# 512-wide products for the high weights of the MLPs, in a trunk of four layers

## The chip, the cores and the metric

The kernel runs on one core of a Trainium2 chip. The metric is the time of one execution on the device in microseconds (us); the profile is one such execution, taken by the hardware profiler. Its engines are TensorE (PE: matmuls into PSUM; PEld are its weight loads), VectorE (DVE), ScalarE (ACT), GpSimd (POOL) and the DMA queues, most of which SyncE (SP) issues.

## The reference

A decoder trunk of four layers over 256 tokens of 1024 features, all in fp32. Every layer is a mixer (S5, FoX attention, GLA, S5 again), an MLP and a gate ("PLE"), each on a normed copy of the residual stream `h`:

```python
def sqrelu_mlp(xn, w1, w2):
    return jnp.square(jax.nn.relu(xn @ w1)) @ w2          # w1: 1024 x 4096, w2: 4096 x 1024

for i in range(DEPTH):
    mixer, j = i % N_MIXERS, i // N_MIXERS
    xn = rmsnorm(h, norm_mix[i])
    y = ...                                               # s5, fox or gla
    h = h + y.astype(h.dtype)
    h = h + sqrelu_mlp(rmsnorm(h, norm_mlp[i]), mlp_w1[i], mlp_w2[i])
    gate = jax.nn.sigmoid(rmsnorm(h, norm_ple[i]) @ ple_gate[i])
    h = h + (p[i] @ ple_proj[i]) * gate
return rmsnorm(h, final_norm)
```

## The kernel before

`h` is kept transposed: features on the 128 partitions, the 256 tokens along the free axis, in four tiles `HH[n]` of 128 x 2 x 256. An fp32 product is made of three products of a narrower type: each operand is split into a high and a low part, and high x high, high x low and low x high are added up in PSUM. `col` issues these three, each 128 features by 256 tokens. `ktiles` holds an input in this form, high part `x[:, 0]` beside low part `x[:, 1]`, 256 tokens each.

Weights arrive as units of 256 x 512: `unit` fetches one (`raw`, on SP's queue), ScalarE casts its high part (`whi`), VectorE subtracts to get the low part (`wlo`). There are 3 buffers for `raw`, and 4 each for `whi` and `wlo`. A unit holds two blocks of 128 input features (`UK`) by four blocks `n` of 128 output features.

An MLP works through 8 blocks `c` of 512 of the 4096 inner features. For each, `dense` multiplies the input by a block of the first weight (four units) into two banks of PSUM with the tag `wk`, `relu2` makes the squared ReLU and splits it into high and low parts, and `second(c - 1)` multiplies the block before it by the second weight (two column halves `cb`, two units each) into four banks `y` (the tag `po` and three of `acc`), which stay open for the whole MLP. At the end `add` multiplies them by the norm's scale `r2` and adds them to `h`. PSUM has eight banks: three `acc`, three `wk`, one `po`, one `mk`. The norm's scale is applied behind the products, so its statistics run beside them: `rstd_rows` takes the mean of squares by a matmul with `mean`, `inverse_root` the root (on GpSimd's power, or a reciprocal on VectorE), `rstd` builds a diagonal tile `diag` on VectorE and spreads it over the partitions by a matmul with `ones`. `further` lets one step of the preparation of the last S5 layer run between blocks of an MLP (`s5_ahead`, in layers 0 to 2).

The gate `ple` calls `dense` with two banks of `acc` for its first column half and two of `wk` for its second, with `rstd_rows` and `rstd` called behind its second and third unit.

In the GLA mixer, `att` is a masked score tile of two chunks of 64 tokens; it is cleared on GpSimd, then the masked part of a PSUM bank is copied in by VectorE, and TensorE multiplies it with `v`. `oss` is GLA's own norm, whose power runs on GpSimd.

A scheduler sets the order on every engine from a simulated timeline, under the rule that a buffer of a pool (`BUFS` gives their numbers) is reused in turn. An engine works through its order strictly in sequence.

Of the kernel before, what the change touches and what calls it, by code (L numbers as in the profile page):

```python
# [18 lines left out]
EPS = 1e-6  # L19
UK = 2  # L20

BUFS = {"raw": 3, "wh": 4, "wl": 4, "x4": 4, "m4": 5, "win": 1, "c4": 6, "qo": 3, "tm": 3, "s2": 10, "a2": 4, "wt": 3, "g2": 3, "s1": 2,
        "acc": 3, "wk": 3, "po": 1, "mk": 1}


# [29 lines left out]
class Trunk:  # L55
# [60 lines left out]
            nc.gpsimd.affine_select(v, v, [[0, 4], [1, 64]], ALU.is_ge, 0, base=0, channel_multiplier=-1)  # L116


    def t1(self, name, shape=(128, T), dt=F32, tag="s1"):
        return self.sc.tile(list(shape), dt, name=name, tag=tag, bufs=BUFS[tag])  # L120

    def t2(self, name, shape=(128, 512), dt=F32, tag="s2"):
        return self.sc.tile(list(shape), dt, name=name, tag=tag, bufs=BUFS[tag])

# [50 lines left out]
    def dense(self, x, w, evac, cbs=(0, 1), scale=None, mid=None, tags=("acc", "acc")):  # L175


        nk = 2 * len(x)
        i = 0
        for cb in cbs:  # L180
            ps = [self.psum((128, 2, T), tags[cb % 2]) for _ in range(2)]
            for k0, (hi, lo) in self.units(w, nk, cb, scale):
                for n in range(4):
                    s = slice(n * 128, (n + 1) * 128)
                    for k in range(UK):

                        self.col(ps[n // 2][:, n % 2], x[(k0 + k) // 2][:, (k0 + k) % 2], hi[:, k, s], lo[:, k, s],
                                 k0 + k == 0 and n % 2 == 0, k0 + k == nk - 1)
# [131 lines left out]
    def rstd(self, rows):  # L320

        nc = self.nc
        ps = self.psum((128, T))
        diag = self.small("diag2", (128, 2, 128), bufs=1)
        for half in range(2):
            nc.vector.tensor_scalar(diag[:, half], self.ident, rows[:, half:half + 1], None, ALU.mult)
        nc.tensor.matmul(ps, self.ones, diag.rearrange("p h t -> p (h t)"), start=True, stop=True)
        r = self.small("rstd", (128, T))
        nc.scalar.copy(r, ps)
        return r  # L330
# [13 lines left out]
    def mlp(self, l):  # L344
        nc, A = self.nc, self.A
        x = self.scaled(DEPTH + l)
        sq = self.squares()
        NC = FF // 512
        s = [None] * NC
        y = [self.psum((128, 2, T), "acc" if i else "po") for i in range(4)]  # L350
        rows = r2 = None

        def add(n):
            t = self.t2("y", (128, 2, T))
            nc.vector.tensor_tensor(t, y[n], r2.unsqueeze(1).broadcast_to([128, 2, T]), ALU.mult)
            nc.vector.tensor_tensor(self.HH[n], self.HH[n], t, ALU.add)

        def second(c):

            for cb in range(2):  # L360
                for k0, (hi, lo) in self.units(A["mlp_w2"][l][c * 512:(c + 1) * 512], 4, cb):
                    for n in range(4):
                        for k in range(UK):
                            self.col(y[cb * 2 + n // 2][:, n % 2], s[c][(k0 + k) // 2][:, (k0 + k) % 2], hi[:, k, n * 128:(n + 1) * 128],
                                     lo[:, k, n * 128:(n + 1) * 128], c == k0 + k == n % 2 == 0, c == NC - 1 and k0 + k == 3)
                if c == NC - 1:
                    for n in range(2):
                        add(cb * 2 + n)

        def further():  # L370
            if self.ahead is not None:
                with self.tc.issue_after(self.last_unit.ins), self.tc.issue_after(self.last_lo.ins), self.tc.issue_after(self.last_mm.ins):
                    next(self.ahead, None)

        for c in range(NC):
            if c:
                further()
            if c == 2:
                rows = self.rstd_rows(sq, -1)
            if c == 3:  # L380
# [12 lines left out]
            further()
            if c:
                second(c - 1)
        second(NC - 1)

    def ple_proj(self, l):

# [146 lines left out]
    def gla(self, l):  # L546
# [657 lines left out]
```

## Time and profile before

| what | value |
|---|---|
| time, median of 3 runs | 1494.93 us (1493.21 to 1495.36) |
| the profiled execution | 1495.53 us, of which its span is 1493.7 us |
| mean granted TensorE clock | 0.977 of full speed |
| TensorE busy | 1424.5 us, 95% of the span |
| VectorE busy | 984.7 us, 66% |
| ScalarE busy | 707.3 us, 47% |
| GpSimd busy | 83.8 us, 6% |
| moved by DMA | 255.28 MB, 171 GB/s in the mean |
| chain of work that ended last | PE 87%, DVE 7%, DMA 2%, issue 2%, ACT 1% |

Busy shares say how much of the span an engine had work; the chain follows the work back from the last instruction, at each step to what released it. A matmul's duration in the trace is longer than the distance to the next one, since they overlap; what one costs is the distance from start to start.

### The profile page before, as it was taken

The numbers are of one execution on the slowest core, as the hardware profiler recorded it, in microseconds if no ns is written. First come the engines' busy times: TensorE is split into PE (matmuls) and PEld (weight loads), VectorE is DVE, ScalarE is ACT, GpSimd is POOL, SyncE is SP. The second block draws the span as 40 slices with busy tenths as digits, with TensorE's granted clock in tenths as the row PEclk, the third lists the DMA queues.
The fourth block names the chain that finished last, engine by engine and source line by source line (L and its number), as shares of the span: only waits on it lengthen the run. The fifth ranks groups of instructions, "written<-read, shape, count | busy, mean of one in ns | idle before, by whom it ended". The sixth has DMA issues, their size and how long they took to land.

```text
span 1493.7 us, 29921 instructions
## 1 busy us (share of the span) xinstructions
PE 1424.5 (95%) x12526; PEld 1369.7 (92%) x12526; DVE 984.7 (66%) x1531; ACT 707.3 (47%) x1006; POOL 83.8 (6%) x142
## 2 busy tenths in 40 slices
PE   8767999999999999999999999999998799999997
PEld 7756999999999889999999679999998799999997
DVE  8972476664776667666775557666486945655564
ACT  3212455444555555544657435545464245444452
POOL 3100000001010000000003100000000000000010
PEclk9878999999999999999999999999999899999998
DMA  7502556656645437676554437666565355655551
GB/s 224 167 13 92 185 170 196 184 179 190 204 140 150 148 100 241 217 214 208 191 182 133 155 112 225 194 206 210 181 229 182 100 179 170 190 181 183 184 183 43
DMA packets 146359, 255.28 MB, mean 171 GB/s; under 512 B 24768, under 2 KB 35296, under 8 KB 146224
## 3 DMA queue, kind: packets, MB, share of 16 engines
q1 hardware_dynamic: 132912, 234.35, 49.9%
q0 software_dynamic: 5248, 17.31, 3.6%
q10 hardware_dynamic: 8064, 1.71, 0.6%
q8 instruction: 98, 1.61, 0.5%
q14 instruction: 37, 0.30, 0.1%
HBM read 242.68 MB, written 7.86 MB: 168 GB/s over the span
## 4 chain that ended last, share of the span: by engine, by line
PE 87%; DVE 7%; DMA 2%; issue 2%; ACT 1%; POOL 0%; ACTq 0%; DVEq 0%; POOLq 0%; SPq 0%
PE acc L171 13%; PE acc L172 13%; PE acc L173 12%; PE wk L171 11%; PE wk L173 11%; PE wk L172 11%; PE po L171 2%; PE po L173 2%; PE po L172 2%; PE acc L206 1%; PE acc L205 1%; PE acc L207 1%; DMA raw<-s_w_glu 1%; DVE R L947 1%; PE wk L505 1%
## 5 line engine op out<-in xcount | busy, mean ns | idle before, releaser
L157 DVE TENSOR_TENSOR wlo<-raw,whi 128x1024 fp32r<-128x1024 f32 x406 | 497.4, 1227 | 373.4 <-ACT whi L155 371.3
L155 ACT CAST whi<-raw 128x1024 fp32r<-128x1024 f32 x406 | 424.2, 1046 | 517.5 <-PE acc L172 254.9
L171 PE MATMUL wk<-x,whi 128*128 128x256 f32 x1184 | 335.9, 286 | 0.0
L173 PE MATMUL wk<-x,wlo 128*128 128x256 f32 x1184 | 335.4, 285 | 0.0
L172 PE MATMUL wk<-x,whi 128*128 128x256 f32 x1184 | 335.4, 284 | 0.0
L172 PEld LDWEIGHTS wk<-x,whi 128*128 128x128 f32 x1184 | 228.7, 193 | 0.2
L173 PEld LDWEIGHTS wk<-x,wlo 128*128 128x128 f32 x1184 | 228.6, 193 | 0.2 <-issue 0.2
L171 PEld LDWEIGHTS wk<-x,whi 128*128 128x128 f32 x1184 | 228.0, 194 | 0.4 <-issue 0.2
L171 PE MATMUL acc<-s,whi 128*128 128x256 f32 x768 | 217.4, 283 | 0.0
L172 PE MATMUL acc<-s,whi 128*128 128x256 f32 x768 | 217.3, 283 | 0.0
L173 PE MATMUL acc<-s,wlo 128*128 128x256 f32 x768 | 217.3, 283 | 0.0
L172 PEld LDWEIGHTS acc<-s,whi 128*128 128x128 f32 x768 | 147.5, 192 | 0.0
L171 PEld LDWEIGHTS acc<-s,whi 128*128 128x128 f32 x768 | 147.5, 192 | 0.0
L173 PEld LDWEIGHTS acc<-s,wlo 128*128 128x128 f32 x768 | 147.5, 192 | 0.0
L171 PE MATMUL acc<-x,whi 128*128 128x256 f32 x352 | 98.9, 288 | 2.9 <-DVE u L1022 2.9
L172 PE MATMUL acc<-x,whi 128*128 128x256 f32 x352 | 101.1, 290 | 0.0
L173 PE MATMUL acc<-x,wlo 128*128 128x256 f32 x352 | 100.4, 287 | 0.0
L171 PE MATMUL po<-s,whi 128*128 128x256 f32 x256 | 72.6, 284 | 0.0
L173 PE MATMUL po<-s,wlo 128*128 128x256 f32 x256 | 72.5, 283 | 0.0
L172 PE MATMUL po<-s,whi 128*128 128x256 f32 x256 | 72.4, 283 | 0.0
L172 PE MATMUL acc<-g,whi 128*128 128x256 f32 x256 | 72.3, 283 | 0.0
L171 PE MATMUL acc<-g,whi 128*128 128x256 f32 x256 | 72.2, 284 | 0.0
(363 smaller groups left out, 2655.4 us busy)
## 6 DMA issues: line engine op xcount, KB each, us to landing
raw<-mlp_w SPq DMA_DIRECT2D x256, 512.0 KB, 3.6
raw<-s_w_glu SPq DMA_DIRECT2D x32, 512.0 KB, 3.6
raw<-ple_gate SPq DMA_DIRECT2D x32, 512.0 KB, 3.3
raw<-fox_w_in SPq DMA_DIRECT2D x24, 512.0 KB, 3.6
raw<-gla_w_in SPq DMA_DIRECT2D x24, 512.0 KB, 3.5
raw<-s_w_out SPq DMA_DIRECT2D x16, 512.0 KB, 3.8
kept<-kept SPq DMA_DIRECT2D x12, 512.0 KB, 5.6
raw<-s_w_in SPq DMA_DIRECT2D x11, 512.0 KB, 3.3
```

The source lines that it names most:

```text
L155: nc.scalar.copy(hi, raw)
L157: self.last_lo = nc.vector.tensor_tensor(lo, raw, hi.bitcast(F32), ALU.subtract)
L171: mm(ps, hi, x[:, 0], start=first, stop=False, skip_group_check=True)
L172: mm(ps, hi, x[:, 1], start=False, stop=False, skip_group_check=True)
L173: self.last_mm = mm(ps, lo, x[:, 0], start=False, stop=last, skip_group_check=True)
L205: mm(ps[half], a[:, 0, t], hi[:, k], start=k0 + k == 0, stop=False)
L206: mm(ps[half], a[:, 0, t], lo[:, k], start=False, stop=False)
L207: mm(ps[half], a[:, 1, t], hi[:, k], start=False, stop=k0 + k == nk - 1)
L505: nc.tensor.matmul(ps[:, i], q[:, half * 128:(half + 1) * 128], k[:, :n * 128], start=True, stop=True)
L947: V.tensor_tensor_scan(flat(R[:, i]), flat(d0), flat(R[:, i]), 0.0, ALU.mult, ALU.add)
```

## The change

`wide` takes the place of `col` in the MLPs: one product of the high weights with both parts of the input, 512 wide, into a whole bank, and one of the low weights with the input's high part, 256 wide, into the first half of the same bank. A block of 512 features so fills four banks instead of two, and the two halves have to be added: in `summed` ScalarE copies the second half to SBUF and VectorE adds the first. A string `MLP` sets the order of the steps (f2 is the first weight's block 2, s21 the second weight's block 2 in column half 1). The second weight's sums are now closed and added to `h` in two groups of four blocks. For the last four blocks of column half 1 the old three products in two banks are kept (`slim`). Two tiles change their place: `diag` and `att` go into the pool with the tag `s2` of ten buffers instead of buffers of their own, and `m4` gets a sixth buffer.

```diff
-BUFS = {"raw": 3, "wh": 4, "wl": 4, "x4": 4, "m4": 5, "win": 1, "c4": 6, "qo": 3, "tm": 3, "s2": 10, "a2": 4, "wt": 3, "g2": 3, "s1": 2,
+BUFS = {"raw": 3, "wh": 4, "wl": 4, "x4": 4, "m4": 6, "win": 1, "c4": 6, "qo": 3, "tm": 3, "s2": 10, "a2": 4, "wt": 3, "g2": 3,
         "acc": 3, "wk": 3, "po": 1, "mk": 1}
...
+MLP = "f0 f1 f2 s00 f3 s10 s20 s30 s01 s11 f4 s21 f5 s31 s40 f6 f7 s50 s60 s70 s41 s51 s61 s71"
...
+    def wide(self, ps, x, hi, lo, k, first, last):
+        mm = self.nc.tensor.matmul
+        for n in range(4):
+            s = slice(n * 128, (n + 1) * 128)
+            v = [x[(k + i) // 2][:, (k + i) % 2] for i in range(UK)]
+            for i in range(UK):
+                mm(ps[n], hi[:, i, s], v[i], start=first and i == 0, stop=False, skip_group_check=True)
+            for i in range(UK):
+                self.last_mm = mm(ps[n][:, 0], lo[:, i, s], v[i][:, 0], start=False, stop=last and i == UK - 1, skip_group_check=True)
...
+    def summed(self, dst, ps):
+        for i, p in enumerate(ps):
+            self.nc.scalar.copy(dst[:, i], p[:, 1])
+            self.nc.vector.tensor_tensor(dst[:, i], p[:, 0], dst[:, i], ALU.add)
+        return dst
...
-        diag = self.small("diag2", (128, 2, 128), bufs=1)
+        diag = self.t2("diag", (128, 2, 128))
...
+        def first(c):
+            s[c] = self.ktiles("s", 2, "m4") + self.ktiles("s", 2, "c4")
+            ps = self.banks([("wk", "acc")[c in (4, 5)]] * 3 + ["mk"])
+            for k, (hi, lo) in self.units(A["mlp_w1"][l], 8, c):
+                self.wide(ps, x, hi, lo, k, k == 0, k == 8 - UK)
+            for n in range(2):
+                v = self.summed(self.t2("relu", (128, 2, T)), ps[2 * n:2 * n + 2])
+                nc.vector.scalar_tensor_tensor(v, v, 0.0, v, ALU.max, ALU.mult)
+                self.split(v, s[c][n][:, :, 0], s[c][n][:, :, 1])
+
+        def second(c, cb):
+            nonlocal y
+            slim = c > 3 and cb == 1
+            if c % 4 == 0:
+                y = self.banks(["wk", "wk"] if slim else [("acc", "wk")[cb]] * 3 + ["po"])
+            for k, (hi, lo) in self.units(A["mlp_w2"][l][c * 512:(c + 1) * 512], 4, cb):
+                first, last = c % 4 == k == 0, c % 4 == 3 and k == 2
+                if slim:
+                    self.pairs(y, s[c], hi, lo, k, first, last)
+                else:
+                    self.wide(y, s[c], hi, lo, k, first, last)
+            if c % 4 == 3:
+                for n in range(2):
+                    t = self.t2("y", (128, 2, T))
+                    v = y[n] if slim else self.summed(t, y[2 * n:2 * n + 2])
+                    nc.vector.tensor_tensor(t, v, r2.unsqueeze(1).broadcast_to([128, 2, T]), ALU.mult)
+                    h = self.HH[cb * 2 + n]
+                    nc.vector.tensor_tensor(h, h, t, ALU.add)
...
-        for c in range(NC):
-            if c:
+        for i, step in enumerate(MLP.split()):
+            c = int(step[1])
+            if step[0] == "f":
+                first(c)
+                if c == 1:
+                    rows = self.rstd_rows(sq, -1)
+                if c == 2:
+                    r2 = self.rstd(rows)
+            else:
+                second(c, int(step[2]))
+            if i and i < 16:
                 further()
...
-            at = self.t1("att", (128, NH, 64))
+            at = self.t2("att", (128, NH, 64))
             nc.gpsimd.memset(at, 0.0)
             nc.vector.copy_predicated(at, self.causal.bitcast(mybir.dt.uint8), pa)
```

The functions `pairs` (the old loop over `col`) and `banks` (a list of PSUM tiles) are not shown. The lines move: of the changed kernel, L208 and L210 are the two products of `wide`, L172 to L174 those of `col`, L218 and L219 the copy and the add of `summed`, L158 the subtraction for `wlo`, L320 the mean of squares, L354 the matmul with `diag`, L386 the squared ReLU, L340 the first step of `inverse_root`.

Three places in the engines' orders. The first is the seam between two blocks of the first weight in layer 0's MLP, on TensorE. Before, block 0's banks are wk_2235 and wk_2236, and block 1 begins with wk_2400 (x_2198 and x_2201 are input tiles):

```order
L173 MATMUL wk_2236<-x_2200,wlo_2300 128x256
L171 MATMUL wk_2235<-x_2201,whi_2329 128x256
L171 MATMUL wk_2236<-x_2201,whi_2329 128x256
L171 MATMUL wk_2400<-x_2198,whi_2404 128x256
L172 MATMUL wk_2400<-x_2198,whi_2404 128x256
L172 MATMUL wk_2235<-x_2201,whi_2329 128x256
L173 MATMUL wk_2235<-x_2201,wlo_2330 128x256
```

In the changed kernel, the seam between f1 (banks wk_2341 to wk_2343 and mk_2344) and f2 (wk_2486, wk_2487, a third one and mk_2489), with the mean of squares between them:

```order
L208 MATMUL wk_2343<-x_2201,whi_2413 128x512 x2
L210 MATMUL wk_2343<-x_2201,wlo_2414 128x256 x2
L208 MATMUL mk_2344<-x_2201,whi_2413 128x512 x2
L210 MATMUL mk_2344<-x_2201,wlo_2414 128x256 x2
L320 MATMUL wk_2449<-mean_91,sq_2218 128x1 x4
L208 MATMUL wk_2486<-x_2198,whi_2492 128x512 x2
L210 MATMUL wk_2486<-x_2198,wlo_2493 128x256 x2
L208 MATMUL wk_2486<-x_2199,whi_2514 128x512 x2
L210 MATMUL wk_2486<-x_2199,wlo_2515 128x256 x2
L208 MATMUL wk_2486<-x_2200,whi_2536 128x512 x2
L210 MATMUL wk_2486<-x_2200,wlo_2537 128x256 x2
L208 MATMUL wk_2487<-x_2198,whi_2492 128x512 x2
```

Before, a third `wk` bank was there for the next block; now all three and `mk` pass from one block to the next, and the first of f2's banks is filled from three units ahead of the others. On VectorE, the changed kernel's rows at the same seam (relu_2433 and relu_2441 are the sums of f1, rrow_2454 the mean's reader):

```order
L158 TENSOR_TENSOR wlo_2493<-raw_2490,whi_2492 128x1024
L158 TENSOR_TENSOR wlo_2515<-raw_2512,whi_2514 128x1024
L158 TENSOR_TENSOR wlo_2537<-raw_2534,whi_2536 128x1024
L219 TENSOR_TENSOR relu_2433<-wk_2341,relu_2433 128x256
L219 TENSOR_TENSOR relu_2433<-wk_2342,relu_2433 128x256
L219 TENSOR_TENSOR relu_2441<-wk_2343,relu_2441 128x256
L219 TENSOR_TENSOR relu_2441<-mk_2344,relu_2441 128x256
L386 SCALAR_TENSOR_TENSOR relu_2433<-relu_2433 128x512
L386 SCALAR_TENSOR_TENSOR relu_2441<-relu_2441 128x512
L340 TENSOR_SCALAR rrow_2454<-wk_2449 128x2
```

The adds, which free f1's banks, stand behind the low parts of f2's first three units, and the mean is read behind them.

The second place is layer 0's gate on TensorE, at the end of its first column half (banks acc_4493 and acc_4494 before, acc_4139 and acc_4140 after; wk_4640 and wk_4286 begin the second half). Before:

```order
L171 MATMUL acc_4494<-x_4465,whi_4602 128x256
L172 MATMUL acc_4494<-x_4465,whi_4602 128x256
L173 MATMUL acc_4494<-x_4465,wlo_4603 128x256
L293 MATMUL wk_4555<-mean_91,sq_4482 128x1 x4
L327 MATMUL wk_4593<-diag2_4594,ones_93 128x256
L171 MATMUL wk_4640<-x_4462,whi_4644 128x256
```

After, where 15 products of `col` stand between the mean and `diag` (nine of them are left out here, at the line of points):

```order
L174 MATMUL acc_4139<-x_4111,wlo_4249 128x256
L320 MATMUL wk_4201<-mean_91,sq_4128 128x1 x4
L172 MATMUL acc_4139<-x_4111,whi_4248 128x256
L173 MATMUL acc_4139<-x_4111,whi_4248 128x256
L174 MATMUL acc_4139<-x_4111,wlo_4249 128x256
...
L172 MATMUL acc_4140<-x_4111,whi_4248 128x256
L173 MATMUL acc_4140<-x_4111,whi_4248 128x256
L174 MATMUL acc_4140<-x_4111,wlo_4249 128x256
L354 MATMUL wk_4239<-diag_4240,ones_93 128x256
L172 MATMUL wk_4286<-x_4108,whi_4290 128x256
```

The mean's matmul has moved ahead of the last 15 products; the matmul with `diag` stays behind them. Layer 3's gate has the same rows.

The third place is GLA's second chunk pair on VectorE (state_9328 before is state_8620 after, o_9390 is o_8682, att_9402 is att_8694). Before:

```order
L643 COPY state_9328<-wk_9370 128x512
L646 SCALAR_TENSOR_TENSOR state_9328<-state_9328,kd_8874,wk_9378 128x256 x2
L622 COPY_PREDICATED att_9402<-causal_1434,wk_9393 128x256
L157 TENSOR_TENSOR wlo_9746<-raw_9743,whi_9745 128x1024
L657 SCALAR_TENSOR_TENSOR o_9390<-wk_9367,oss_9383,gn_8792 128x256 x2
```

After:

```order
L672 COPY state_8620<-wk_8662 128x512
L675 SCALAR_TENSOR_TENSOR state_8620<-state_8620,kd_8166,wk_8670 128x256 x2
L158 TENSOR_TENSOR wlo_9038<-raw_9035,whi_9037 128x1024
L686 SCALAR_TENSOR_TENSOR o_8682<-wk_8659,oss_8675,gn_8084 128x256 x2
L651 COPY_PREDICATED att_8694<-causal_1434,wk_8685 128x256
L695 TENSOR_TENSOR silu_8846<-silu_8846,o_8682 128x512
```

The masked copy into `att` has moved behind the `o` products. On GpSimd, after (before, both clears of `att` stand among the first 30 rows of the program):

```order
L682 TENSOR_SCALAR oss_8649<-oss_8649 128x2
L683 TENSOR_TENSOR oss_8649<-oss_8649,mhalf_89 128x2
L682 TENSOR_SCALAR oss_8675<-oss_8675 128x2
L683 TENSOR_TENSOR oss_8675<-oss_8675,mhalf_89 128x2
L650 MEMSET att_8694 128x256
L682 TENSOR_SCALAR oss_8711<-oss_8711 128x2
```

The second clear has moved behind the power of oss_8675.

## Rows read from the trace of the kernel before

**Rows 1.** The page's first part: busy us (share of the span) and number of instructions of each engine.

```profile
PE 1424.5 (95%) x12526; PEld 1369.7 (92%) x12526; DVE 984.7 (66%) x1531; ACT 707.3 (47%) x1006; POOL 83.8 (6%) x142
```

**Rows 2.** Windows of the span, one for the MLP of each layer, 0 to 3: from and to, length, then busy us (instructions) of PE, PEld, DVE, ACT and POOL, the granted clock, the DMA share and GB/s.

```profile
211.40:396.00 184.60, 184.60 (x1538) 184.30 (x1537) 120.96 (x222) 93.52 (x117) 5.67 (x9) 1.00 0.61 189
552.00:737.00 185.00, 185.00 (x1556) 184.30 (x1555) 130.46 (x167) 93.08 (x117) 8.60 (x16) 1.00 0.67 211
896.00:1088.00 192.00, 192.00 (x1638) 190.00 (x1637) 126.96 (x159) 95.09 (x120) 7.49 (x14) 1.00 0.64 201
1265.00:1449.00 184.00, 184.00 (x1535) 183.95 (x1534) 107.48 (x118) 90.22 (x109) 6.22 (x8) 1.00 0.59 184
```

**Rows 3.** What TensorE waited for: line, the instruction that released it, us in total, times, longest us.

```profile
PE wk L327 <- DVE diag L326: 5.3, 2, 2.6
...
PE wk L632 <- DVE att L622: 0.5, 1, 0.5
```

**Rows 4.** TensorE's timeline at the start of layer 0's MLP, the first and the fourteenth of a row of products 256 wide: start, duration, instruction.

```profile
211.41 0.28 PE L171 MATMUL wk<-x,whi 128*128 128x256 f32 x1
...
212.97 0.28 PE L172 MATMUL wk<-x,whi 128*128 128x256 f32 x1
```

**Rows 5.** TensorE's timeline in the FoX layer, where products 512 wide (L205 to L207) and 256 wide (L171 to L173) meet; from 456.60 to 462.27 there are 26 of the wide ones, with the two rows that hold two counted as such.

```profile
453.28 0.28 PE L173 MATMUL acc<-x,wlo 128*128 128x256 f32 x1
453.40 0.63 PE L205 MATMUL acc<-whi,x 128*128 128x512 f32 x2
...
456.60 0.39 PE L206 MATMUL acc<-wlo,x 128*128 128x512 f32 x1
...
462.27 0.39 PE L207 MATMUL acc<-whi,x 128*128 128x512 f32 x1
...
466.73 0.39 PE L207 MATMUL acc<-whi,x 128*128 128x512 f32 x1
466.95 0.28 PE L171 MATMUL acc<-x,whi 128*128 128x256 f32 x1
```

**Rows 6.** VectorE's groups by line and shape: busy us in total, mean ns of one, idle us before them.

```profile
L157 DVE TENSOR_TENSOR wlo<-raw,whi 128x1024 fp32r<-128x1024 f32 x406 | 497.4, 1227 | 373.4 <-ACT whi L155 371.3 <-PE acc L173 0.9
...
L355 DVE TENSOR_TENSOR y<-acc,rstd 128x512 f32<-128x512 f32 x12 | 8.2, 684 | 0.3
...
L240 DVE TENSOR_TENSOR o<-wk,o 128x256 fp32r<-128x256 f32 x8 | 3.2, 420 | 1.6 <-ACT o L239 1.5
```

**Rows 7.** ScalarE's groups, with the same columns.

```profile
L155 ACT CAST whi<-raw 128x1024 fp32r<-128x1024 f32 x406 | 424.2, 1046 | 517.5 <-PE acc L172 254.9 <-PE wk L172 150.3 <-issue 30.5
L389 ACT ACTIVATE s<-relu 128x512 fp32r<-128x512 f32 x64 | 40.4, 631 | 1.7
...
L387 ACT ACTIVATE relu<-wk 128x512 f32<-128x512 f32 x64 | 38.1, 595 | 13.9 <-PE wk L173 13.7
...
L239 ACT CAST glu<-sg 128x512 fp32r<-128x512 f32 x8 | 4.7, 617 | 0.0
...
L329 ACT COPY rstd<-wk 128x256 f32<-128x256 f32 x12 | 4.4, 369 | 12.9 <-PE wk L327 12.8
```

**Rows 8.** The timeline of layer 0's gate; idle time before an instruction and its releaser in brackets. L282 is the last sum of squares, L293 the mean, L317 the power, L326 and L327 `diag` and its matmul.

```profile
405.18 0.68 DVE L282 TENSOR_TENSOR sq<-sq 128x512 f32<-128x512 f32 x1
...
409.13 0.95 PE L293 MATMUL wk<-mean,sq 128*128 128x1 f32 x8
...
410.34 1.22 DVE L157 TENSOR_TENSOR wlo<-raw,whi 128x1024 fp32r<-128x1024 f32 x1
410.43 1.71 POOL L317 TENSOR_TENSOR rrow<-rrow,mhalf 128x2 f32<-128x2 f32 x1 [11.64 <-DVE rrow L313]
412.18 0.48 DVE L326 TENSOR_SCALAR diag<-ident,rrow 128x128 f32<-128x128 f32 x2 [0.62 <-POOL rrow L317]
...
412.71 0.70 PE L327 MATMUL wk<-diag,ones 128*128 128x256 f32 x2 [2.62 <-DVE diag L326]
...
413.06 0.47 PE L171 MATMUL wk<-x,whi 128*128 128x256 f32 x1
...
417.13 0.28 PE L173 MATMUL wk<-x,wlo 128*128 128x256 f32 x1
```

**Rows 9.** TensorE's timeline in layer 3's gate, from the first product behind the wait for `diag` to the one 25 products later.

```profile
1466.26 0.77 PE L171 MATMUL wk<-x,whi 128*128 128x256 f32 x1
...
1471.82 0.28 PE L172 MATMUL wk<-x,whi 128*128 128x256 f32 x1
```

**Rows 10.** Windows at the end of the GLA mixer and in layer 3's gate, with the columns of rows 2.

```profile
868.00:874.00 6.00, 4.43 (x29) 3.27 (x29) 4.46 (x11) 2.88 (x10) 1.49 (x3) 1.00 0.09 18
...
1466.00:1471.50 5.50, 5.50 (x25) 5.32 (x25) 3.79 (x6) 2.52 (x6) 0.00 (x0) 0.50 0.00 0
```

**Rows 11.** GLA's second chunk pair: the timelines of PE, DVE and POOL, and GpSimd's group of the clears of `att` (mean ns behind the busy us), which ran at 5.5 and 5.8 us.

```profile
857.25 0.64 PE L632 MATMUL wk<-v,att 64*64 64x256 f32 x2 [0.53 <-DVE att L622]
...
856.75 0.44 DVE L622 COPY_PREDICATED att<-causal,wk 128x256 f32<-128x256 uint8 x1
...
859.16 0.88 DVE L657 SCALAR_TENSOR_TENSOR o<-wk,oss,gn 128x256 f32<-128x256 f32 x2 [0.86 <-POOL oss L654]
...
858.44 0.69 POOL L654 TENSOR_TENSOR oss<-oss,mhalf 128x2 f32<-128x2 f32 x1
...
L621 POOL MEMSET att<- 128x256 f32 x2 | 0.6, 343 | 0.0
```

More of the change, by code (lines that the diff above doesn't have):

```diff
@@ L116, in masks @@
             nc.gpsimd.affine_select(v, v, [[0, 4], [1, 64]], ALU.is_ge, 0, base=0, channel_multiplier=-1)
-    def t1(self, name, shape=(128, T), dt=F32, tag="s1"):
-        return self.sc.tile(list(shape), dt, name=name, tag=tag, bufs=BUFS[tag])
     def t2(self, name, shape=(128, 512), dt=F32, tag="s2"):
@@ L182, in dense @@
             for k0, (hi, lo) in self.units(w, nk, cb, scale):
[L183 to L188, printed above, removed]
+                self.pairs(ps, x, hi, lo, k0, k0 == 0, k0 + UK == nk)
                 if mid and i in mid:
@@ L193, in dense, with pairs, banks @@
                 evac(cb * 2 + n, ps[n])
+    def pairs(self, ps, x, hi, lo, k, first, last):
+        for n in range(4):
+            s = slice(n * 128, (n + 1) * 128)
+            for i in range(UK):
+                self.col(ps[n // 2][:, n % 2], x[(k + i) // 2][:, (k + i) % 2], hi[:, i, s], lo[:, i, s], first and i == n % 2 == 0,
+                         last and i == UK - 1)
+    def wide(self, ps, x, hi, lo, k, first, last):
+        mm = self.nc.tensor.matmul
+        for n in range(4):
+            s = slice(n * 128, (n + 1) * 128)
+            v = [x[(k + i) // 2][:, (k + i) % 2] for i in range(UK)]
+            for i in range(UK):
+                mm(ps[n], hi[:, i, s], v[i], start=first and i == 0, stop=False, skip_group_check=True)
+            for i in range(UK):
+                self.last_mm = mm(ps[n][:, 0], lo[:, i, s], v[i][:, 0], start=False, stop=last and i == UK - 1, skip_group_check=True)
+    def banks(self, tags):
+        return [self.psum((128, 2, T), t) for t in tags]
+    def summed(self, dst, ps):
[3 more added lines that the diff above has]
+        return dst
     def rows(self, x, w, cb, evac):
@@ L347, in mlp @@
         sq = self.squares()
[L348 to L368, printed above, removed]
+        s = {}
@@ new lines, in mlp @@
+        y = r2 = None
+        def first(c):
[7 more added lines that the diff above has]
+                self.split(v, s[c][n][:, :, 0], s[c][n][:, :, 1])
```

17 lines of the change are left out of this document (removed).

## The prediction

> **What bounds the kernel now.** Read the engines' shares first: TensorE is busy in 95% of the span [rows 1], so time is gained by giving it less to do or by closing its gaps. Next the windows over the four MLPs, where the change is made: in each TensorE is busy for the whole window, at full granted clock, while VectorE has 107 to 130 us of work in 184 to 192 and ScalarE about 93 [rows 2]. An MLP has 512 pairs of a weight tile and an input tile (8 blocks x 8 x 4 in either weight), three products each, and 1536 x 0.120 us are 184.3 us: the window. Then the list of what TensorE waited for [rows 3]: nothing in an MLP; of the waits there, the change touches those for `diag` (5.3 us, twice 2.6, in the gates of layers 0 and 3) and for `att` (0.5 us).
>
> **What a pair costs.** The 128x256 products start 0.1200 us apart (13 steps from 211.41 to 212.97) [rows 4]. The 128x512 products that the FoX layer has today start 0.2268 us apart (25 steps from 456.60 to 462.27), and where the two widths meet each takes its own time: 0.12 us from a 256 to the 512 behind it, 0.22 from a 512 to the 256 behind it [rows 5]. Twice the width is 0.0132 us less than twice the time. So a pair now costs 3 x 0.1200 = 0.3600 us, and 0.2268 + 0.1200 = 0.3468 after. 448 of an MLP's 512 pairs become wide (the last four blocks of the second weight keep three products in their second column half: 64 pairs), in four MLPs 1792: 1792 x 0.0132 = 23.7 us less. The array still takes as many columns; only the share that each instruction costs beyond its columns is saved.
>
> The Trainium skill (TensorE: Matmul & The Clock Gate, Back-to-back issue gap) gives the spacing at full clock as the columns at 2.4 GHz plus about 2.5 ns. By it only 2.5 ns would go with each instruction and the term would be an estimated 4.5 us. The trace disagrees: 120.0 and 226.8 ns are each about 13 ns above the columns, and I go by the trace.
>
> **What it adds on the other engines.** A block now has four banks, each with two halves to be added. That is 44 additions per MLP (8 blocks x 4; 12 for the three groups with four banks) by a 128x256 copy on ScalarE and a 128x256 add on VectorE; nearest rows 0.420 us for the add (L240, a 256 from PSUM) [rows 6] and 0.369 for the copy (L329) [rows 7]. With eight more 128x512 operations, for a sum that is taken in two groups (0.684 each), VectorE gets 44 x 0.420 + 8 x 0.684 = 24 us more per MLP, ScalarE 44 x 0.369 + 16 casts x 0.617 less 16 x (0.595 + 0.631) = 6.5 us. The fullest MLP, layer 1's, would have 154 us on VectorE and 100 on ScalarE under some 179 of TensorE [rows 2]. As sums both stay hidden, and cost nothing as long as 179 is the largest; what can be seen is a bank that is not free in time.
>
> **Hand-offs of banks.** Before, a block had two of three `wk` banks, and the second weight's four stayed open for the whole MLP. Now f0, f1 and f2 each take all of `wk` and `mk`. In a block's last unit a bank gets two pairs, 0.69 us, so the first is complete 2.1 us before the block ends. To free it takes a copy and an add, 0.79 us, and at worst a cast (1.05) and a subtraction (1.23) that are just running ahead of them in the two queues: 3.07 us [rows 6, 7]. So it is between 1.3 us early and 1.0 late, 0.2 early in the middle; the banks behind it come every 0.42 us, faster than TensorE fills them. This happens at f0 to f1, f1 to f2, f6 to f7, and for `po` at s30 to s01 and s31 to s40. The dearest is f1 to f2: the mean of squares stands between them and takes the first bank, VectorE's order puts three subtractions ahead of f1's four adds, and the bank of the statistic is read only behind four adds and two maxima (4 x 0.42 + 2 x 0.68 = 3.0 us); TensorE's order answers with three units of f2's first bank (2.1 us) ahead of the third bank. I take 0.9 us there, 0.6 for the other four together: 1.5 per MLP, 6.0 in all. Bounds: nothing, and 5 x 1.0 x 4 = 20 us. Blocks queued behind such a wait come later by as much; nothing else reads them at once.
>
> **Moves outside the MLP.** Two tiles change their pool, and with that the scheduler's order.
> First the gates of layers 0 and 3. Today the mean of squares is the last thing before the wait: it starts at 409.13, the power on GpSimd takes 1.71 us, `diag` starts at 412.18, and TensorE has idled 2.62 us at 412.71 [rows 8]; layer 3 likewise [rows 9]. Behind the gap the products come 0.21 us apart: 20 of them from 413.06 to 417.13 and 25 from 1466.26 to 1471.82, which at 0.120 would be 1.67 and 2.56 us less; the granted clock was 0.50 behind the second [rows 8 to 10], that is the lower level, 1.2 GHz. The new order sets the mean 15 products earlier, and 15 x 0.120 = 1.8 us of work then lie in the gap: 0.8 us of wait is left. Behind 1.57 us of idle time in the window 868 to 874 the clock stayed at 1.00 [rows 10], so I expect no fall. Gain 2 x 1.8 + 1.67 + 2.56 = 7.8 us; bounds 0 and 7.8. The last sum of squares is done at 405.86 [rows 8], so nothing new is waited for.
>
> Then GLA. Today both clears of `att` run on GpSimd before 6 us [rows 11]. In the new order the second stands behind the second power of `oss`, which ends at 859.13, and on VectorE the masked copy comes behind the two `o` products, 859.16 to 860.04. So `att` is there at 860.48 instead of 857.19, and TensorE, whose next work reads it, goes on 3.3 us later [rows 11]. The gap grows from 0.53 to 3.8 us, longer than the 2.62 that were followed by a fall of the clock, and I add the smaller of those two losses, 1.7. Cost 5.0 us; bounds 3.3 and 5.9 (with the larger loss).
>
> The sixth `m4` buffer lets a transfer start earlier, and DMA's share of 0.67 in the fullest MLP grows by 3% with the shorter time: no term.
>
> **Sum** against the profiled execution, 1495.5: -23.7 - 7.8 + 5.0 + 6.0 = -20.5, 1475.0. That execution was 0.6 us above the median of the runs: 1474.4, say 1474.
>
> **Rivals.**
> *All hand-offs hidden.* Speaks for it: the middle case above is early. 1474 - 6 = 1468, or 1466 where the clock stays up in GLA. 0.05.
> *The gates keep their wait.* If the mean is ready no sooner than now, because VectorE reads it late, 7.8 us do not come: 1482. Against it: today a subtraction of 1.22 us stands right behind that read and is done before the power is [rows 8], so VectorE has room. 0.10.
> *Slower: banks bind.* VectorE is then 86% full in layer 1's MLP, its queue is in order, and every add waits behind subtractions of 1.23 us. From (23.7 + 7.8 - 5.0) / 4 = 6.6 us of waits per MLP on, the change loses. If in each of the 24 steps one add of 0.42 us lay open, that were 10 us per MLP: 1474 + 4 x 8.5 = 1508. Against it: only five places hand a bank straight on. 3 to 6.6 us per MLP (1480 to 1494) 0.08; above 6.6, 0.05.
> *The change doesn't save.* A wide product set between narrow ones could cost two narrow ones, 0.240 us. Then 23.7 us do not come, and 1498 is left. The transitions in rows 5 speak against it, but are only two. 0.04, half of it beyond 0.2% slower. The skill's spacing, TensorE page as above, would give an estimated 1493.6.
>
> **How the numbers follow.** The forecast, hand-offs of up to 3 us per MLP around 1474, has the remaining 0.68; its own range is 1468 to 1480. The range 1466 to 1486 adds the hidden hand-offs, the gates without gain, and the lower half of the dear hand-offs. About 3 us, 0.2%, can be told from no change. Faster: 0.68 + 0.05 + 0.10 + 0.07 = 0.90; same 0.03; slower 0.07.
>
> **What would show it.** In the MLP windows, 178 to 181 us instead of 184.6, TensorE still full; 512-wide starts 0.227 apart, 256-wide 0.120; VectorE near 145 to 154. In the list of waits: `diag` below 1 us and no half clock behind it; a wait for `att` of 3 to 4 us; for banks (the adds of `summed`) 1 to 2 us per MLP, most of it behind f1. I am wrong if wide starts lie at 0.24, if waits for the adds pass 3 us per MLP, or if a wait that isn't named here appears in a mixer.

## The result and the profile after

The changed kernel takes 1497.13 us (median of 17 runs) against 1493.78 for the kernel before on the same chips: ratio 1.0019, 95% interval 1.0010 to 1.0028. It is slower by 0.2%, where 1474 was forecast. The profiled execution has a span of 1497.0 us against 1493.7.

The page's first part, which answers to [rows 1]:

```profile
PE 1416.0 (95%) x10734; PEld 1273.0 (85%) x10734; DVE 1055.2 (70%) x1739; ACT 721.3 (48%) x1118; POOL 85.7 (6%) x142
```

TensorE has 8.5 us less to do, and its share of the span is as before: what it was spared, it waits elsewhere. Where, the starts of the first and the last product of each MLP tell; they cut either span into six parts:

| part | before, us | after, us | difference |
|---|---|---|---|
| start to the first MLP (S5) | 211.4 | 211.6 | +0.2 |
| the four MLPs | 753.5 | 747.5 | -6.0 |
| MLP 0 to MLP 1 (gate 0, FoX) | 152.9 | 151.3 | -1.6 |
| MLP 1 to MLP 2 (gate 1, GLA) | 157.1 | 173.0 | +15.9 |
| MLP 2 to MLP 3 (gate 2, S5) | 175.4 | 175.5 | +0.1 |
| last MLP to the end (gate 3, final norm) | 43.3 | 38.1 | -5.2 |

The MLPs gained 6.0 us, the two parts with the gates of layers 0 and 3 6.8, and the part with GLA lost 15.9.

Windows over the MLPs after, cut at those products (columns as in [rows 2]); the line behind them is the sum of the same windows before, from 211.41 to 397.49 and so on:

```profile
211.57:395.43 183.86, 181.50 (x1103) 161.00 (x1102) 137.79 (x273) 97.25 (x142) 8.62 (x12) 1.00 0.61 190
546.74:736.12 189.38, 185.19 (x1134) 164.10 (x1133) 151.88 (x224) 97.20 (x148) 8.59 (x16) 0.99 0.66 208
909.11:1100.56 191.45, 189.19 (x1205) 167.00 (x1203) 147.24 (x215) 98.03 (x148) 7.47 (x14) 1.00 0.65 204
1276.04:1458.89 182.85, 180.97 (x1099) 160.69 (x1098) 124.72 (x169) 93.32 (x135) 8.97 (x8) 1.00 0.60 185
sum 747.54, PE 736.85 PEld 652.79 DVE 561.63 ACT 385.80 POOL 33.66; mean PE 184.21 PEld 163.20 DVE 140.41 ACT 96.45 POOL 8.42
...
sum 753.52, PE 753.52 PEld 750.46 DVE 493.73 ACT 373.98 POOL 27.98; mean PE 188.38 PEld 187.61 DVE 123.43 ACT 93.49 POOL 6.99
```

TensorE's work in them fell by 16.7 us (753.52 to 736.85), but it idles 10.7 us (747.54 - 736.85), where it didn't idle at all. VectorE got 17 us more per MLP.

What TensorE waited for, after; the first two rows are for banks (L219 is the add that frees one), and answer to no row of before, the last two answer to [rows 3]:

```profile
PE wk L208 <- DVE relu L219: 8.3, 5, 3.1
...
PE wk L320 <- DVE relu L219: 2.4, 3, 1.1
...
PE wk L661 <- DVE att L651: 3.3, 1, 3.3
...
PE wk L354 <- DVE diag L353: 0.9, 1, 0.9
```

Of the first row's 8.3 us, 7.6 are at f6 to f7, once in every layer (1.6, 3.1, 1.5 and 1.4 us); the fifth wait, 0.8 us in layer 2, is at f1 to f2, where the second row's 2.4 us are too. So f1 to f2 cost 3.1 us in all.

The gap before `att` is 3.3 us long, 2.8 more than before, and yet that part is 15.9 us longer. Before, TensorE's next pair of products there followed the one at 857.25 [rows 11] so:

```profile
857.82 0.65 PE L634 MATMUL wk<-state,e 128*64 128x256 f32 x2
```

After, TensorE's timeline at that place, then VectorE's and GpSimd's, and windows behind the gap (columns as in [rows 2]):

```profile
854.85 0.63 PE L648 MATMUL wk<-e,e 128*64 128x64 f32 x12
858.81 1.11 PE L661 MATMUL wk<-v,att 64*64 64x256 f32 x2 [3.33 <-DVE att L651]
859.85 1.11 PE L663 MATMUL wk<-state,e 128*64 128x256 f32 x2
860.90 1.11 PE L661 MATMUL wk<-v,att 64*64 64x256 f32 x2
...
883.83 0.56 PE L173 MATMUL acc<-o,whi 128*128 128x256 f32 x1
...
888.40 0.28 PE L174 MATMUL acc<-o,wlo 128*128 128x256 f32 x1
...
857.54 0.88 DVE L686 SCALAR_TENSOR_TENSOR o<-wk,oss,gn 128x256 f32<-128x256 f32 x2 [0.86 <-POOL oss L683]
858.33 0.43 DVE L651 COPY_PREDICATED att<-causal,wk 128x256 f32<-128x256 uint8 x1
...
857.45 0.31 POOL L650 MEMSET att<- 128x256 f32 x1
...
858.80:888.00 29.20, 27.34 (x73) 13.54 (x74) 7.41 (x17) 3.92 (x14) 2.38 (x5) 0.50 0.09 30
...
890.00:900.00 10.00, 10.00 (x86) 10.00 (x85) 5.24 (x7) 3.12 (x4) 0.00 (x0) 1.00 0.39 109
```

The granted clock is 0.50, the lower of its two levels, from the first product behind the wait until about 888. A pair of GLA's products starts every 1.04 us there; before, they started every 0.57 us. That lasts 29 us. The clock is back at 888.4, behind 4.6 us of an unbroken row of 128x256 products (from 883.83). As the prediction read it from the new order, the masked copy ran behind the two `o` products; the clear itself was done at 857.76, before the copy's turn came.

The dearest seam, f6 to f7 in layer 1's MLP, on TensorE, ScalarE and VectorE:

```profile
680.29 0.40 PE L210 MATMUL mk<-x,wlo 128*128 128x256 f32 x2
683.79 1.22 PE L208 MATMUL wk<-x,whi 128*128 128x512 f32 x2 [3.10 <-DVE relu L219]
...
679.86 1.05 ACT L156 CAST whi<-raw 128x1024 fp32r<-128x1024 f32 x1 [4.52 <-DMA raw<-mlp_w]
681.10 1.04 ACT L156 CAST whi<-raw 128x1024 fp32r<-128x1024 f32 x1 [0.20 <-DMA raw<-mlp_w]
682.05 0.91 ACT L218 COPY relu<-wk 128x256 f32<-128x256 f32 x3
...
680.94 2.46 DVE L158 TENSOR_TENSOR wlo<-raw,whi 128x1024 fp32r<-128x1024 f32 x2 [3.33 <-ACT whi L156]
683.32 1.08 DVE L219 TENSOR_TENSOR relu<-wk,relu 128x256 f32<-128x256 f32 x3
```

f6's first bank was complete by about 679.4 and f6 ended near 680.6. Its copy was ready to run, but stood on ScalarE behind two casts, and those waited for their fetch: 4.52 us, until 679.86, and 0.20 more, until 681.10. The copies ran at 682.05, the adds at 683.32, behind two subtractions that had waited for the casts. Two casts and two subtractions were not "just running"; they were late, and held what stood behind them. In layers 2 and 3 the first of the two casts waited for its fetch too (3.3 and 3.2 us), and the second behind it for VectorE and TensorE (1.3 and 1.5 us).

### The profile page after: what moved, and what is told of

It reads as the page before. It is cut to its first block, busy times and chain, and to the rows that moved or that the text cites. A ratio compares the mean times of both kernels' runs of the same rounds, so it can differ in the third digit from the quotient of the medians.

```text
span 1497.0 us, 26616 instructions
## 1 busy us (share of the span) xinstructions
PE 1416.0 (95%) x10734; PEld 1273.0 (85%) x10734; DVE 1055.2 (70%) x1739; ACT 721.3 (48%) x1118; POOL 85.7 (6%) x142
## 4 chain that ended last, share of the span: by engine, by line
PE 82%; DVE 8%; DMA 4%; ACT 3%; issue 2%; ACTq 0%; POOL 0%; SPq 0%; DVEq 0%; POOLq 0%
PE wk L208 11%; PE acc L208 9%; PE acc L172 6%; PE acc L173 6%; PE acc L174 6%; PE wk L210 5%; PE acc L210 4%; PE wk L172 4%; PE wk L173 4%; PE wk L174 4%; PE mk L208 3%; PE po L208 3%; DVE wlo L158 2%; PE mk L210 2%; PE po L210 1%
## 5 line engine op out<-in xcount | busy, mean ns | idle before, releaser
L158 DVE TENSOR_TENSOR wlo<-raw,whi 128x1024 fp32r<-128x1024 f32 x406 | 494.8, 1228 | 305.3 <-ACT whi L156 298.7
L208 PE MATMUL wk<-x,whi 128*128 128x512 f32 x576 | 181.2, 399 | 8.3 <-DVE relu L219 8.3
L210 PEld LDWEIGHTS wk<-x,wlo 128*128 128x128 f32 x576 | 106.3, 189 | 23.1 <-issue 0.2
L208 PE MATMUL acc<-s,whi 128*128 128x512 f32 x384 | 118.8, 395 | 0.0
L210 PE MATMUL wk<-x,wlo 128*128 128x256 f32 x576 | 112.9, 280 | 0.0
L172 PE MATMUL acc<-x,whi 128*128 128x256 f32 x352 | 99.6, 288 | 4.6 <-DVE u L1051 2.9
L208 PEld LDWEIGHTS wk<-x,whi 128*128 128x128 f32 x576 | 91.2, 190 | 11.9 <-DVE relu L219 9.2
L173 PE MATMUL acc<-x,whi 128*128 128x256 f32 x352 | 100.4, 288 | 0.0
L174 PE MATMUL acc<-x,wlo 128*128 128x256 f32 x352 | 100.1, 286 | 0.0
L210 PEld LDWEIGHTS acc<-s,wlo 128*128 128x128 f32 x384 | 70.6, 188 | 15.9
L208 PE MATMUL mk<-x,whi 128*128 128x512 f32 x256 | 81.3, 395 | 0.0
L210 PE MATMUL acc<-s,wlo 128*128 128x256 f32 x384 | 74.9, 280 | 0.0
L172 PEld LDWEIGHTS acc<-x,whi 128*128 128x128 f32 x352 | 67.5, 194 | 6.3 <-issue 4.1
L174 PE MATMUL wk<-s,wlo 128*128 128x256 f32 x256 | 72.4, 283 | 0.0
L173 PE MATMUL wk<-s,whi 128*128 128x256 f32 x256 | 72.4, 283 | 0.0
L172 PE MATMUL wk<-s,whi 128*128 128x256 f32 x256 | 72.4, 283 | 0.0
L173 PE MATMUL acc<-g,whi 128*128 128x256 f32 x256 | 72.3, 283 | 0.0
L172 PE MATMUL acc<-g,whi 128*128 128x256 f32 x256 | 72.2, 284 | 0.0
L174 PE MATMUL acc<-g,wlo 128*128 128x256 f32 x256 | 71.7, 283 | 0.0
L174 PEld LDWEIGHTS acc<-x,wlo 128*128 128x128 f32 x352 | 68.2, 194 | 0.1
L173 PEld LDWEIGHTS acc<-x,whi 128*128 128x128 f32 x352 | 68.0, 194 | 0.2
```

The source lines that it names most:

```text
L158: self.last_lo = nc.vector.tensor_tensor(lo, raw, hi.bitcast(F32), ALU.subtract)
L172: mm(ps, hi, x[:, 0], start=first, stop=False, skip_group_check=True)
L173: mm(ps, hi, x[:, 1], start=False, stop=False, skip_group_check=True)
L174: self.last_mm = mm(ps, lo, x[:, 0], start=False, stop=last, skip_group_check=True)
L208: mm(ps[n], hi[:, i, s], v[i], start=first and i == 0, stop=False, skip_group_check=True)
L210: self.last_mm = mm(ps[n][:, 0], lo[:, i, s], v[i][:, 0], start=False, stop=last and i == UK - 1, skip_group_check=True)
```

## The experiments

Theory A: GLA's loss is one late tile, 3.3 us of waiting plus the lower clock behind it; the MLPs' missing gain is waiting at the seams, where a copy or an add stands behind a late fetch. The rivals: GLA is late for another reason (B), VectorE or the steps themselves bind at the seams (C, E).

**e1: `att` cleared once, early.**

```diff
+        ats = self.t2("att", (128, 2, NH, 64))
+        nc.gpsimd.memset(ats, 0.0)
         for half in range(2):
...
-            at = self.t2("att", (128, NH, 64))
-            nc.gpsimd.memset(at, 0.0)
+            at = ats[:, half]
```

> The changed kernel with one edit: both halves of att lie in one tile, cleared once ahead of the loop, so that the second clear no longer stands behind the power. Theory A (the late att costs GLA its 15.9 us: 3.3 us of waiting, and the rest because TensorE goes on at half clock): the stretch from the end of layer 1's MLP to the first product of layer 2's is 157 to 159 us instead of 173, at full clock, and the time is 1480 to 1483 us against 1497. Rival B (GLA is slower for another reason, its transfers or the new order of the MLP before it): only the wait of 3.3 us goes, the stretch is about 169 us, the time 1493 to 1494.

Measured: 1485.06 us, ratio to before 0.9935 (0.9916 to 0.9955). The part between the MLPs of layers 1 and 2, as a window, and the wait:

```profile
734.13:892.03 157.90, 154.37 (x1007) 129.55 (x1006) 100.69 (x142) 88.16 (x140) 25.63 (x28) 1.00 0.50 148
...
PE wk L662 <- DVE att L652: 0.5, 1, 0.5
```

157.9 us at full clock: 15.1 of the 15.9 us are gone with one tile's place. The time is 12 us below the change, with the part in A's range and the median 2 us above it. B falls. TensorE's waits for banks are 8.5 us in this profile, where the MLPs are those of the change with its 10.7: they vary that much.

**e2: the same tile moved in the kernel before.**

```diff
-            at = self.t1("att", (128, NH, 64))
+            at = self.t2("att", (128, NH, 64))
```

> The kernel before with one edit: att in the pool s2, as in the change. Theory A: the same 15.9 us appear in the kernel before, 1508 to 1511 us against 1494, with a wait for att of 3 to 4 us and half clock behind it. Rival B: 1494 to 1498.

Measured: 1509.86 us, ratio 1.0106 (1.0091 to 1.0121). The waits and a window behind the gap:

```profile
PE wk L632 <- DVE att L622: 3.3, 1, 3.3
...
857.00:888.00 31.00, 26.35 (x82) 12.64 (x79) 10.38 (x22) 5.12 (x19) 3.87 (x8) 0.57 0.10 34
```

The same wait and the same low clock, with the MLPs of before. The part is 170.3 us long, 13.1 more than before, and another 2.9 us came in the S5 layer behind it (178.3 against 175.4); that part's length differs between the kernels here (174.3 to 178.3), and why was not followed. As A has it.

**e5: the gap filled with work that nothing needs.**

```diff
+            if half:
+                pf = self.psum(tag="mk")
+                with self.tc.issue_after(last.ins):
+                    for i in range(8):
+                        nc.tensor.matmul(pf[:, :256], self.ones, ku[0][:, :256], start=True, stop=True)
```

> The changed kernel with eight 128x256 products in plain fp32 (ones by ku, some 0.4 us each, 3.4 us) put on TensorE behind GLA's second scores, into the mk bank, which is idle there; nothing reads their result, and att stays as late as in the change. Theory A (of GLA's 15.9 us, 3.3 are the wait itself, and 12.5 come from the half clock that follows the gap): without a gap the clock stays at 1.00, the stretch between the MLPs of layers 1 and 2 is 160 to 162 us instead of 173, the time 1484 to 1486 against 1497. Rival B (the clock falls for what TensorE does behind the gap, or GLA is late for another reason): stretch 172 to 174, 1496 to 1498.

Measured: 1488.12 us, ratio 0.9961 (0.9950 to 0.9973). TensorE's timeline and windows of the part and of the stretch behind the gap:

```profile
854.25 3.72 PE L653 MATMUL mk<-ku,ones 128*128 128x256 f32 x16
857.90 0.64 PE L666 MATMUL wk<-v,att 64*64 64x256 f32 x2
858.48 0.65 PE L668 MATMUL wk<-state,e 128*64 128x256 f32 x2
...
734.99:896.47 161.48, 158.28 (x1024) 132.44 (x1023) 100.41 (x142) 88.09 (x140) 25.27 (x29) 1.00 0.48 144
853.00:870.00 17.00, 16.43 (x81) 8.62 (x80) 6.96 (x14) 3.19 (x12) 2.38 (x5) 1.00 0.10 32
```

`att` is as late as in the change, but the clock stays at 1.00 and the part takes 161.5 us, 11.5 less. So 4.3 us are the late tile and what else changed there (161.5 - 157.1), and 11.5 the clock that TensorE loses where the gap is idle. The median is 2 us above A's range: the last S5 layer took 178.1 us here.

**e3: the seams f1 to f2 and f6 to f7 taken apart.**

```diff
-MLP = "f0 f1 f2 s00 f3 s10 s20 s30 s01 s11 f4 s21 f5 s31 s40 f6 f7 s50 s60 s70 s41 s51 s61 s71"
+MLP = "f0 f1 s00 f2 s10 f3 s20 s30 s01 s11 f4 s21 f5 s31 s40 f6 s50 f7 s60 s70 s41 s51 s61 s71"
```

> The changed kernel with another order of the steps: f1 s00 f2 s10 f3 and f6 s50 f7 in place of f1 f2 s00 f3 and f6 f7 s50, so that no block of the first weight but f1 follows directly on one that holds the same banks. Theory A (the MLPs lose what they gain at the seams f1 to f2 and f6 to f7, 10.7 us of waiting for the adds): these waits fall below 3 us, the four MLPs are 8 to 10 us shorter together, the time is 1487 to 1490 against 1497. Rival C (VectorE is too full, and what is not waited for at these seams is waited for at others): waits for adds stay near 10 us, 1494 to 1498.

Measured: 1486.88 us, ratio 0.9958 (0.9943 to 0.9973). The waits for adds, and the sum of the four MLP windows:

```profile
PE po L208 <- DVE y L219: 0.5, 1, 0.5
PE wk L208 <- DVE relu L219: 0.5, 1, 0.5
...
sum 739.05, PE 735.30 PEld 651.69 DVE 561.22 ACT 387.42 POOL 34.26; mean PE 183.82 PEld 162.92 DVE 140.31 ACT 96.85 POOL 8.56
```

The waits for adds are 1.0 us, the MLPs 8.5 us shorter, with VectorE as full as in the change (561.2 us). C falls: it isn't VectorE's load. Of the 3.75 us that TensorE still idles there (739.05 - 735.30), 1.6 are a wait for one block's split in layer 0.

**e4: both.** The edits of e1 and e3 together.

> Both edits, of e1 and e3. Theory A: the two add up, 1471 to 1475 us, below both kernels. Rival C: as e1 alone, 1480 to 1483.

Measured: 1471.36 us, ratio 0.9847 (0.9830 to 0.9863). They add up: the two gains against the change, 12.1 and 10.2 us, would give 1474.8.

**e6: a fourth buffer for the fetched weights.**

```diff
-BUFS = {"raw": 3, ... "s2": 10, ...
+BUFS = {"raw": 4, ... "s2": 8, ...
```

> The changed kernel with a fourth buffer for the fetched weights (raw 3 to 4, and s2 10 to 8 to make room). Theory A (at the seams the copy stands on ScalarE behind a cast that waits for its fetch, 1.2 to 4.5 us before f7): with an earlier fetch TensorE's waits for the adds fall from 10.7 us to 3 to 6, the time to 1489 to 1493. Rival C (the cast, the subtraction, the copy and the add themselves take that long): waits 9 to 11 us, 1496 to 1498.

Measured: 1477.36 us, ratio 0.9890 (0.9875 to 0.9905).

```profile
PE wk L320 <- DVE relu L219: 2.2, 3, 1.1
...
PE wk L208 <- DVE relu L219: 0.8, 1, 0.8
...
sum 737.41, PE 734.40 PEld 651.41 DVE 561.71 ACT 387.62 POOL 34.51; mean PE 183.60 PEld 162.85 DVE 140.43 ACT 96.90 POOL 8.63
...
664.66 1.05 ACT L156 CAST whi<-raw 128x1024 fp32r<-128x1024 f32 x1 [1.68 <-DMA raw<-mlp_w]
666.30 1.09 ACT L218 COPY relu<-wk 128x256 f32<-128x256 f32 x3 [0.59 <-PE wk L210]
```

The wait at f6 to f7 vanishes in all four layers (7.6 us to none) with the order of the steps as it was; the one at f1 to f2 stays (3.1 to 3.0: the 0.8 in the second row is layer 2's). The last two rows are the dear seam of layer 1: the same casts stand ahead of the first copy there, the last of them still waits 1.7 us for its fetch, and yet the copy then waits 0.6 us for TensorE to fill the bank. So f7's seam was a late fetch, as A has it; f1's seam is not. The time fell further than either theory said, because the first S5 layer became 8.8 us shorter (202.7 us to the first MLP, against 211.6): e10 takes that up.

**e8: no copy and no addition.**

```diff
-            self.nc.scalar.copy(dst[:, i], p[:, 1])
-            self.nc.vector.tensor_tensor(dst[:, i], p[:, 0], dst[:, i], ALU.add)
+            self.nc.vector.tensor_copy(dst[:, i], p[:, 0])
```

> The changed kernel where summed only copies the first half of a bank on VectorE; ScalarE's copy and the addition are left out, so the products of the high weights with the input's low part are missing from the output. Theory A (what a bank waits for at the seams is a late fetch, which holds the cast and with it the subtraction ahead of the add): the waits for banks fall by no more than the copies' 0.4 us at each of 8 seams, to 7 or 8 us, time 1493 to 1496. Rival E (ScalarE's copy behind the cast is what is late): below 3 us, 1487 to 1490.

Measured: 1484.01 us, ratio 0.9937 (0.9922 to 0.9952). TensorE waits for no bank at all in the MLPs:

```profile
sum 733.30, PE 733.30 PEld 650.51 DVE 560.51 ACT 335.26 POOL 33.08; mean PE 183.32 PEld 162.63 DVE 140.13 ACT 83.82 POOL 8.27
```

Here A's number fails and E's holds (below 3 us; the time is even below E's range). But more than the copy is gone. VectorE at the dear seam of layer 1:

```profile
673.33 1.23 DVE L158 TENSOR_TENSOR wlo<-raw,whi 128x1024 fp32r<-128x1024 f32 x1 [2.83 <-ACT whi L156]
674.47 0.42 DVE L218 COPY relu<-wk 128x256 f32<-128x256 f32 x1
674.80 1.22 DVE L158 TENSOR_TENSOR wlo<-raw,whi 128x1024 fp32r<-128x1024 f32 x1
```

VectorE's order has changed: the first bank is read ahead of the second subtraction, and no longer behind both. The casts also came earlier against f6: the second began 1.4 us before f6's last row of products (673.59 and 674.95), and in the change 0.8 us behind it (681.10 and 680.29). So e8 shows that these waits vanish without copy and add; how much of them lay in ScalarE's queue and how much in VectorE's, it doesn't tell. What e6 shows stands by itself: with an earlier fetch the wait is gone.

**e7: the change's buffers in the kernel before.** `diag` in s2, six buffers of m4, `att` in one tile as in e1.

> The kernel before with the change's buffers alone: diag in s2, six buffers of m4, and att in one tile cleared once (so that it isn't late). Theory A (as the prediction had it, the new pools move the mean of squares in the gates of layers 0 and 3): waits for diag below 2 us, 1486 to 1488. Rival D (the MLP's new order moves it, since the first column half is added to h four steps earlier): the waits for diag stay at 5.3 us, 1493 to 1496.

Measured: 1494.57 us, ratio 1.0006 (0.9997 to 1.0015), and

```profile
PE wk L327 <- DVE diag L326: 5.3, 2, 2.6
```

D holds. The pools are worth nothing by themselves, and the gates' gain is not theirs: what is left of the change is the MLP itself, its products and its new order. That it is the earlier sum of the first column half is argued, not shown.

**e9 and e10: what the fourth buffer is worth, with and without the change.** e9 has the edits of e1, e3 and e6; e10 is the kernel before with that of e6.

> The changed kernel with the edits of e1, e3 and e6 together (att in one tile, the other order of steps, raw in four buffers and s2 in eight). Theory A: no wait for adds above 1 us, GLA's stretch 157 to 158 us, and the S5 layer ahead of the first MLP 8 us shorter as in e6: 1460 to 1464 us. Rival F (the fourth buffer and the new order take away the same waits, and the S5 layer's gain was chance): 1469 to 1473, as e4.

> The kernel before with raw in four buffers and s2 in eight. Theory A (the 8 us that e6 gained ahead of the first MLP are the S5 layer's own, nothing of the wide products): 1484 to 1488 against 1494, the MLPs as before at 753 us together. Rival F: 1492 to 1496.

Measured: e9 1462.60 us, ratio 0.9789 (0.9774 to 0.9803); e10 1486.73, ratio 0.9953 (0.9936 to 0.9969). The MLP windows of e9 and of e10:

```profile
sum 733.35, PE 733.35 PEld 651.25 DVE 562.50 ACT 389.54 POOL 35.17; mean PE 183.34 PEld 162.81 DVE 140.63 ACT 97.39 POOL 8.79
...
sum 753.48, PE 753.48 PEld 750.42 DVE 494.14 ACT 372.96 POOL 28.06; mean PE 188.37 PEld 187.60 DVE 123.53 ACT 93.24 POOL 7.01
```

The S5 layer's 8 us come without the wide products too. GLA's part of e9 is 159.4 us, 1.4 above what was expected. With a fourth buffer in either kernel, and the change freed of `att` and the two seams, the change is worth 24.1 us (1486.73 to 1462.60), 20.1 of them in the MLPs, where TensorE now waits for nothing. e9 is the fastest of all.

**e11: the price of a pair.** e4 with each 512-wide product followed by its 256-wide one.

```diff
             for i in range(UK):
                 mm(ps[n], hi[:, i, s], v[i], ...)
-            for i in range(UK):
                 self.last_mm = mm(ps[n][:, 0], lo[:, i, s], v[i][:, 0], ...)
```

> Kernel e4 with the products of a unit in the order high, low, high, low instead of high, high, low, low. Theory A (each change of width costs a little, which would be why two pairs take 0.697 us and not the 0.694 that the rows of before give): two pairs take about 0.700 us, the MLPs 1 us each longer. Rival G (the price lies in the 512-wide product itself): 0.697 us, no difference.

Measured: 1471.46 us in one run (e4: 1471.36). TensorE's timeline of e11, the first and the last of 14 pairs, and of e8, which has the change's order, the first and the last of six groups of two pairs:

```profile
1295.22 0.40 PE L208 MATMUL po<-s,whi 128*128 128x512 f32 x1
...
1299.81 0.40 PE L208 MATMUL wk<-x,whi 128*128 128x512 f32 x1
```

```profile
1299.62 0.63 PE L208 MATMUL acc<-s,whi 128*128 128x512 f32 x2
...
1303.10 0.62 PE L208 MATMUL acc<-s,whi 128*128 128x512 f32 x2
```

A pair takes 4.59 / 13 = 0.3531 us where the widths alternate and 3.48 / 10 = 0.3480 in the change's order; the sum of the single spacings was 0.3468. Changes of width do cost, as A has it, and more than expected (two pairs 0.706 against 0.700). Layer 3's MLP, where neither kernel waits, is 182.1 us here and 180.4 in e4. The other MLPs hold waits in e4, and the whole time shows no difference.

## Why the prediction was wrong

Two terms missed by about as much: GLA's by 10.9 us (15.9 against 5.0) and the MLPs' by 11.7 (a gain of 6.0 against 23.7 - 6.0 = 17.7). Without either of the two the change is faster than the kernel before (e1, e3).

**GLA: the path was right, the clock's price was not.** The cause was foreseen, the masked copy that came late behind the power and the `o` products, and so was the wait, nearly: a gap of 3.8 us was forecast and 3.3 came. Wrong was the step "I add the smaller of those two losses, 1.7": the clock's price was taken from the gates, where products of full size follow the gap, 25 of them in 5.6 us [rows 9], and the clock was back after 4 to 6 us. In GLA products of 64 rows follow, and the clock stayed down for 29 us: 11.5 us by e5, up to 13.1 by the change itself (15.9 - 2.8), not 1.7. The bound of 5.9 was worked out from the same two rows and was no bound. With 16 in place of 5 the sum would have been 1485, and the MLPs' miss makes up the rest.

**The hand-offs: mechanism right, place and size off.** 10.7 us were waited against 6.0. For f1 to f2 3.6 us stood in the sum (4 x 0.9), and 3.1 came. For the other seams 2.4 stood there, and 7.6 came, all at f6 to f7. The step that failed is "at worst a cast (1.05) and a subtraction (1.23) that are just running": it gave instructions ahead in the queue their durations only, not their own waits. [rows 7] showed that the casts idle for TensorE, and the fetch behind them was never followed. e3 took nearly all of these waits away, and e6 those at f6 to f7.

**The products: a bit less than the sum.** 23.7 us were forecast; in e8 and e9, where nothing is waited for, 20.2 and 20.1 came (753.5 to 733.3). A pair takes 0.348 us and not 0.3468, 1.2 ns for 1792 pairs or 2.2 us; that a change of width costs (e11) fits this, and where the other 1.3 us went was not followed. In the change itself TensorE's work fell by 16.7 us only, in part since waits also cost at their end. Behind the 3.1 us of layer 1 the clock was down for 3 us, about 1.6 us of work lost:

```profile
683.80:687.00 3.20, 3.20 (x10) 2.72 (x11) 3.17 (x6) 1.00 (x3) 0.00 (x0) 0.51 0.90 306
```

The Trainium skill's figure (TensorE: Matmul & The Clock Gate, Back-to-back issue gap), 2.5 ns beyond the columns, which that section gives for an isolated product, would make an estimated 4.5 us here and does not agree: the 20.2 us of e8 are 11.3 ns a pair.

**VectorE and ScalarE.** 24 us more per MLP were forecast for VectorE and 17.0 came ((561.6 - 493.7) / 4). A single add takes the 0.42 us of the forecast (a mean of 417 ns in layer 1's MLP), but operations that stand right behind each other overlap: three adds take 1.08 us (above), not 1.26. ScalarE got 3.0 instead of 6.5. That both stay hidden as sums held.

**The gates.** 7.8 us forecast, 6.8 came; the wait for `diag` is 0.9 us in one gate and not in the list for the other, and the granted clock is 1.00 in the windows behind (410 to 414, and 1469 to 1475): as forecast. But the cause named, the tiles' new pool, was wrong (e7); the number came out all the same, since it was read from the new order itself.

**The rivals.** "Slower: banks bind" was given 0.05 with a point of 6.6 us per MLP; they bound at 2.7, most of it at f6 to f7 and not behind f1. The kernel became slower through the two together: GLA, a term that had been seen and priced at a third, and MLPs that gained a third of what was forecast. One wait came in a mixer that nobody had named, 3.5 us for `decay` in the last S5 layer; that part's length stayed as it was (175.5 against 175.4).

## What to carry to other kernels

A gap's price is its length plus what the clock loses behind it, and here that differed with the work that follows: 29 us at half clock where products of 64 rows stand behind the gap, 4 to 6 where full ones do. Which property of that work made the difference, no run tests; but look at what stands behind a new gap before taking a loss from another place. Follow each instruction that stands ahead in a queue to what it waits for itself; an operation put on an engine that casts fetched weights inherits the lateness of the fetch. And look up a moved tile's place in every queue: moving one small tile cost 15.9 us, and 1792 cheaper pairs saved 20.2.

## What the runs showed of the hardware that was not expected

TensorE counted as busy in the profile for 27.3 of 29.2 us behind GLA's gap, and the granted clock stayed at 0.50 all the time; with the gap filled (e5) the same products ran at 1.00. So the lower level can hold over a long stretch in which the profile shows the engine almost always busy. In the change it ended 4.6 us into an unbroken row of 128x256 products. Two 512-wide products followed by two 256-wide take 0.696 us, and in alternation 0.706: a change of width costs some nanoseconds, which the two single transitions in [rows 5] did not show.
